# The down projection of a gated FFN, from a plain tiled product to Strassen's seven products, with its operands passed through DRAM

## The chip, the cores and the metric

The kernel runs on one core of one Trainium2 chip, in one launch. The metric is the device time of an execution in microseconds (us); lower is better. The engines are PE (TensorE, matrix products), DVE (VectorE), ACT (ScalarE), POOL (GpSimd) and SP (SyncE, which here only issues DMAs). An engine works through its own instructions in order; semaphores order the engines among themselves.

## The reference

One layer of a hybrid block over x of 1024 rows by 1024 columns, all in float32. What comes before the part that is changed is a combined input projection, forgetting attention (8 heads), an RWKV-7 recurrence (8 heads), their gated merge and an output projection. Then:

```
h2 = rmsnorm(x, g_ffn)
u = causal_dwconv(h2 @ w_up, conv_w, conv_b)              # w_up: 1024 x 5632, conv of width 3 along the rows
x = x + (gelu(u[..., :2816]) * u[..., 2816:]) @ w_down    # w_down: 2816 x 1024
ple_gate = sigmoid(rmsnorm(x, g_ple) @ w_ple_gate)        # w_ple_gate: 1024 x 1024
out = x + ple_gate * (p @ w_ple_up)
```

## The kernel before

Every float32 product is made of three matmuls of rounded parts: an operand is split into H (a cast to the fp32r format, on ACT) and L (the rest, a subtraction on DVE or POOL), and H·H, H·L and L·H are added up in PSUM. A function named `split` or `up_halve` makes such a pair.

The code gives instructions in a written order and with generators that take turns (`interleave`); a scheduler then sets each engine's order from dependences and its own estimate of times, so an instruction can be issued ahead of one that is written before it. Tiles are taken from pools; a tile of the same tag and place waits for the last reader of the one before it.

The stages in order of time: the first norm and projections (to about 380 us), attention head pair by head pair beside the next pair's projections (`fox_att`, `fox_z`, to about 660 us), the recurrence's chain beside gates (to about 960 us), the merge and the output projection `wout` with the second norm (to about 1110 us), the up projection `ffn_up` (to 1545 us), the down projection `ffn_down` (to 1814 us), and the gate projection `ple` (to the end).

The up projection is Strassen's scheme already: for each of 22 blocks f of 128 columns (and its partner f + 22) seven products over 512 rows and half the depth (`up_mul`, four steps of three matmuls of 128x512 each), from sums of weight quarters that POOL makes (`up_s12`, `up_s3`) and sums of the normed rows. DVE and ACT combine the products to c0 and c1, run the convolution (`up_conv`: one ACT and two DVE operations), gelu and the product u0·u1 (`up_m`), and store the block, 128 x 1024, to DRAM (`md`).

The down projection takes the 22 blocks in pairs. `down_load` brings two blocks of md and their rows of w_down from DRAM on SP's queue, `down_split` splits them, and `down` goes over eight row tiles and two column halves: six matmuls of 128x512 into one PSUM bank, then a DVE addition of the bank to the row tile of x (L1234, or L1236 for two banks). x was stored to DRAM (`x1d`) before the up projection and is loaded back by POOL's queue as the stage starts. In the last turn, three blocks are taken at once, and the third norm (`norm`: square and root on ACT, scaling on DVE, eight transposes on PE in `turn`, one split) follows two row tiles behind; the first gate products begin while the last norms run.

PSUM has eight banks of 128x512: in the up projection two "ps" and six "pu", in the down projection two "ps" and three "zt" of two banks each.

Of the kernel before, what the change touches and what calls it, by code (L numbers as in the profile page):

```python
# [29 lines left out]
NFB = DFF // P  # L30
RMS_EPS = 1e-6
# [53 lines left out]
class Net:  # L85
# [931 lines left out]
    def wout_w(self, ap, gp):  # L1017

        nc = self.nc
        W = []  # L1020
        for i in range(2):
            raw = gp.tile([P, 4, 256], F32, name=f"gB{i}", tag=f"gB{i}", bufs=1)
            nc.gpsimd.dma_start(raw, self.a["w_out"][i * 512:i * 512 + 512, 0:256].rearrange("(k p) n -> p k n", p=P))
# [51 lines left out]
    def up_load(self, f):  # L1075
        pool, tag = (self.wp, "wr") if f % 2 == 0 else (self.up, "rr")
# [90 lines left out]
    def up_m(self, f, c0, u1, q=None):  # L1167
        nc = self.nc
# [3 lines left out]
        (q or nc.sync).dma_start(self.md[f], u0)  # L1172

    def ffn_up(self, first, last):
# [9 lines left out]
        for f in range(NFB):  # L1184
            more = f + 1 < NFB
            c0 = up.tile([P, T], F32, name="c0", tag="c0", bufs=2)
            c1 = up.tile([P, T], F32, name="c1", tag="c1", bufs=2)
            m1 = mul(f, "a11", "b11") if f else first[0]
            nc.scalar.copy(c0[:, lo], m1)
            if f:  # L1190
                u1 = self.up_conv(before[1], NFB + f - 1)
            else:
                self.up_load(1)
            m2 = mul(f, "a12", "b21") if f else first[1]
            if f:
                self.up_m(f - 1, before[0], u1)
                self.up_rest(f)
# [3 lines left out]
            if f + 2 < NFB:  # L1201
                self.up_load(f + 2)
            m5 = mul(f, "s1", "t1")
            if more:
                self.up_a1(f + 1)
                self.up_s12(f + 1)
# [6 lines left out]
            if more:  # L1213
                self.up_halve(self.A[f + 1]["s2"], self.sums[f + 1][1][:])
                self.up_halve(self.A[f + 1]["s1"], self.sums[f + 1][0][:])
# [3 lines left out]
            if more:  # L1219
                self.up_s3(f + 1)  # L1220
            add(c0[:, hi], c0[:, hi], m3)  # L1221
            before = c0, c1
        u1 = self.up_conv(before[1], 2 * NFB - 1)
        self.up_m(NFB - 1, before[0], u1, nc.scalar)

    def down(self, ms, tb, z=None):

        ts = slice(tb * P, tb * P + P)
        for n in range(2):
            cs = slice(n * 512, n * 512 + 512)  # L1230
            ps = self.ps.tile([P, 512], F32, name="ps", tag="ps") if z is None else z[:, cs]
            self.mm3(ps, [((mh[:, ts], ml[:, ts]), (W[0][:, cs], W[1][:, cs])) for (mh, ml), W in ms])
            if z is None:
                self.nc.vector.tensor_add(self.x1[tb][:, cs], self.x1[tb][:, cs], ps)  # L1234
        if z is not None:
            self.nc.vector.tensor_add(self.x1[tb], self.x1[tb], z)  # L1236

    def down_first(self, pool):

        nc = self.nc  # L1240
        M = pool.tile([P, 4, T], F32R, name="hah", tag="hah", bufs=1)
        ms = []
        for f in range(2):
            W = self.wload(self.a["w_down"][f * P:f * P + P, :])
            raw = self.up.tile([P, T], F32, name="rr", tag="rr", bufs=2)
            nc.sync.dma_start(raw, self.md[f])
            mh, ml = M[:, 2 * f], M[:, 2 * f + 1]
            self.split(raw, mh, ml)
            ms.append(((mh, ml), (W[0][:, 0, :], W[1][:, 0, :])))
        return ms  # L1250

    def down_load(self, g):
        f0 = 2 * g
        raws = [self.wo.tile([P, 2, T], F32, name="vr", tag="vr", bufs=1)]
        self.nc.sync.dma_start(raws[0], self.a["w_down"][f0 * P:(f0 + 2) * P, :].rearrange("(k p) n -> p k n", p=P))
        for f in (f0, f0 + 1):
            raws.append(self.fp.tile([P, T], F32, name="uc", tag="uc", bufs=3))
            self.nc.sync.dma_start(raws[-1], self.md[f])
        return raws

    def down_split(self, g, raws, pools):
        H = self.wo.tile([P, 2, T], F32R, name="vh", tag="vh", bufs=2)
        L = self.wo.tile([P, 2, T], F32R, name="vl", tag="vl", bufs=2)
        if g < 10:
            pool, name = pools[g % 4]
            M = pool.tile([P, 4, T], F32R, name=name, tag=name, bufs=1)
        ms = []
        for j in range(2):
            f = 2 * g + j
            if f <= NFB - 4:  # L1270
                mh, ml = M[:, 2 * j], M[:, 2 * j + 1]
            else:
                mh, ml = [self.fp.tile([P, T], F32R, name=n, tag=n, bufs=3) for n in ("mh", "ml")]
                mh, ml = mh[:], ml[:]
            self.split(raws[1 + j], mh, ml)
            self.split(raws[0][:, j], H[:, j], L[:, j])
            ms.append(((mh, ml), (H[:, j], L[:, j])))
        return ms

    def ffn_down(self, ms, pools):  # L1280

        for g in range(1, NFB // 2):
            raws = self.down_load(g)
            for tb in range(NTB):
                if g == NFB // 2 - 1:
                    self.down(ms[:1], tb, self.zt.tile([P, T], F32, name="zt", tag="zt") if tb % 2 else None)
                else:

                    z = g == 1 and (tb < 3 or tb % 2)
                    self.down(ms, tb, self.zt.tile([P, T], F32, name="zt", tag="zt") if z else None)  # L1290
                if tb == 2:
                    after = self.down_split(g, raws, pools)
            ms = ms[1:] + after if g == NFB // 2 - 1 else after
        return ms
# [45 lines left out]
    def ple(self, q, tb, hT, pu, W):  # L1340
# [16 lines left out]
        elif tb % 4 == 3:  # L1357
            nc.gpsimd.dma_start(self.out[(tb - 3) * P:(tb + 1) * P, cs].rearrange("(b p) n -> p b n", p=P), self.sg)
# [7 lines left out]
    def body(self, stop):  # L1366
# [83 lines left out]
        self.tlag = 12.0  # L1450

# [20 lines left out]
        close_fwp()  # L1472
        close_gwp()
# [75 lines left out]
        self.wo, _ = self.pool("wo", side="right")  # L1549
# [3 lines left out]
        for cs in (slice(0, 256), slice(256, D)):  # L1553
            for tb in range(NTB):
                nc.gpsimd.dma_start(self.x1[tb][:, cs], self.a["x"][tb * P:tb * P + P, cs])
# [18 lines left out]
        self.md = self.tc.dram_tile([NFB, P, T], F32, name="md")  # L1574
# [27 lines left out]
        close_ps = self.pools(("ps", 2), ("pu", 6))  # L1602
# [31 lines left out]
        for tag, n, bufs in (("u", T, 2), ("s1r", 512, 1), ("s2r", 512, 1), ("s4r", 512, 1), ("s3r", 512, 1),  # L1634
                             ("c0", T, 2), ("c1", T, 2), ("rr", T, 2)):
            self.up.tile([P, n], F32, name=tag, tag=tag, bufs=bufs)
        ms = []
        self.ffn_up(first, lambda: ms.extend(self.down_first(hA)))
# [72 lines left out]
```

## Time and profile before

| | |
|---|---|
| runs | 1911.43, 1912.30, 1915.68 us; median 1912.3 |
| the profiled execution's own time | 1914.04 us |
| its span, first to last instruction | 1912.3 us |
| PE busy | 1843.1 us, 10999 matmuls |
| granted TensorE clock, mean | 0.987 |
| moved by DMA | 201.27 MB |

Rows of the timeline read: start, duration, engine, line of the kernel, operation, output<-inputs, count; in brackets, the idle time of the engine before it and what ended that. Rows that group instructions read: line, engine, operation, tiles, count, busy time and mean of one in ns, idle time before. Rows by stretch give each engine's busy time (and instructions), PE's granted clock, the share of the DMA engines' time and the GB/s moved. PEld is PE's weight load, which runs beside its matmuls.

### The profile page before, as it was taken

The numbers are of one execution on the slowest core, as the hardware profiler recorded it, in microseconds if no ns is written. First come the engines' busy times: TensorE is split into PE (matmuls) and PEld (weight loads), VectorE is DVE, ScalarE is ACT, GpSimd is POOL, SyncE is SP. The second block draws the span as 40 slices with busy tenths as digits, with TensorE's granted clock in tenths as the row PEclk, the third lists the DMA queues.
The fourth block names the chain that finished last, engine by engine and source line by source line (L and its number), as shares of the span: only waits on it lengthen the run. The fifth ranks groups of instructions, "written<-read, shape, count | busy, mean of one in ns | idle before, by whom it ended". The sixth has DMA issues, their size and how long they took to land.

```text
span 1912.3 us, 28229 instructions
## 1 busy us (share of the span) xinstructions
PE 1843.1 (96%) x10999; PEld 1507.3 (79%) x10999; DVE 1215.8 (64%) x2457; ACT 747.6 (39%) x1191; POOL 247.8 (13%) x195
## 2 busy tenths in 40 slices
PE   6999999899999999999999999999999979999999
PEld 5877779789897766666779978888888867778899
DVE  7446764676656434453362698888888867676843
ACT  4544333576757411222541353444343431121331
POOL 3000001000000000000054023333333200000000
PEclk9999999899999999999999999999999989999999
DMA  4356554322212355343654132222222273231041
GB/s 157 89 143 163 141 130 96 83 65 56 69 37 79 94 130 146 115 141 96 218 171 140 78 88 87 82 75 85 82 77 89 88 252 111 89 110 45 26 130 56
DMA packets 258429, 201.27 MB, mean 105 GB/s; under 512 B 77464, under 2 KB 227694, under 8 KB 258295
## 3 DMA queue, kind: packets, MB, share of 16 engines
q1 hardware_dynamic: 189943, 158.26, 27.3%
q10 hardware_dynamic: 65024, 28.61, 5.8%
q0 software_dynamic: 3328, 12.58, 1.9%
q8 instruction: 87, 1.43, 0.3%
q14 instruction: 47, 0.39, 0.1%
HBM read 142.23 MB, written 57.18 MB: 104 GB/s over the span
## 4 chain that ended last, share of the span: by engine, by line
PE 62%; DVE 4%; DMA 2%; ACT 2%; issue 1%; POOL 0%; SPq 0%; DVEq 0%; POOLq 0%; ACTq 0%
PE pu L1153 7%; PE pu L1155 7%; PE pu L1154 7%; PE zt L227 3%; PE zt L226 3%; PE zt L228 3%; PE ps L226 3%; PE ps L228 3%; PE ps L227 3%; PE zt L235 2%; PE zt L236 2%; PE zt L985 2%; PE zt L237 2%; PE zt L987 2%; PE zt L986 2%
## 5 line engine op out<-in xcount | busy, mean ns | idle before, releaser
L1234 DVE TENSOR_TENSOR x<-x,ps 128x512 f32<-128x512 f32 x142 | 96.4, 686 | 60.3 <-PE ps L228 60.1
L206 ACT CAST vh<-vr 128x1024 fp32r<-128x1024 f32 x32 | 32.1, 1047 | 184.0 <-PE ps L228 170.9
L206 ACT CAST wh<-wr 128x1024 fp32r<-128x1024 f32 (+1 forms) x45 | 40.2, 895 | 145.3 <-PE zt L236 85.6
L235 PE MATMUL zt<-hah,wh 128*128 128x512 f32 (+1 forms) x200 | 80.8, 405 | 0.0
L236 PE MATMUL zt<-hal,wh 128*128 128x512 f32 (+1 forms) x200 | 79.0, 395 | 0.0
L235 PE MATMUL zt<-hbh,wh 128*128 128x512 f32 (+1 forms) x200 | 78.7, 393 | 0.0
L237 PE MATMUL zt<-hah,wl 128*128 128x512 f32 (+1 forms) x200 | 78.2, 391 | 0.0
L236 PE MATMUL zt<-hbl,wh 128*128 128x512 f32 (+1 forms) x200 | 78.0, 390 | 0.0
L237 PE MATMUL zt<-hbh,wl 128*128 128x512 f32 (+1 forms) x200 | 77.6, 388 | 0.0
L1164 DVE SCALAR_TENSOR_TENSOR u<-c,par,u 128x1022 f32<-128x1022 f32 x44 | 73.6, 1672 | 0.8
L1163 DVE SCALAR_TENSOR_TENSOR u<-c,par,u 128x1023 f32<-128x1023 f32 x44 | 68.6, 1560 | 7.5 <-ACT u L1162 7.5
L1153 PE MATMUL pu<-hah,wh 128*128 128x512 f32 x176 | 70.3, 399 | 0.0
L1154 PE MATMUL pu<-hal,wh 128*128 128x512 f32 x176 | 69.8, 397 | 0.0
L1155 PE MATMUL pu<-hah,wl 128*128 128x512 f32 x176 | 69.7, 396 | 0.0
L1162 ACT ACTIVATE u<-c,par 128x1024 f32<-128x1024 f32 x44 | 54.7, 1242 | 28.3 <-DVE c L1221 28.3
L226 PE MATMUL zt<-vh,mh 128*128 128x256 f32 (+1 forms) x202 | 61.8, 306 | 0.0
L824 ACT ACTIVATE pr<-pr,st 128x128 f32<-128x128 f32 (+3 forms) x64 | 49.7, 777 | 30.7 <-DVE st L823 30.1
L228 PE MATMUL zt<-vh,ml 128*128 128x256 f32 (+1 forms) x202 | 61.2, 303 | 0.0
L227 PE MATMUL zt<-vl,mh 128*128 128x256 f32 (+1 forms) x202 | 61.0, 302 | 0.0
L848 DVE TENSOR_TENSOR pl<-tr,ph 128x512 fp32r<-128x512 f32 (+1 forms) x80 | 50.0, 633 | 14.5 <-ACT ph L847 13.9
L207 DVE TENSOR_TENSOR wl<-wr,wh 128x1024 fp32r<-128x1024 f32 (+1 forms) x36 | 39.5, 1100 | 24.0 <-ACT wh L206 23.7
L847 ACT CAST ph<-tr 128x512 fp32r<-128x512 f32 (+1 forms) x80 | 42.2, 542 | 19.7 <-PE tr L842 16.8
(549 smaller groups left out, 5767.6 us busy)
## 6 DMA issues: line engine op xcount, KB each, us to landing
X<-Xd SPq DMA_DIRECT2D x28, 448.0 KB
wr<-in_w_up SPq DMA_DIRECT2D x22, 512.0 KB
rr<-in_w_up SPq DMA_DIRECT2D x22, 512.0 KB
wr<-in_w_in ACTq DMA_DIRECT2D x21, 512.0 KB
md<-u SPq DMA_DIRECT2D x21, 512.0 KB
vr<-in_w_down SPq DMA_DIRECT2D x10, 1024.0 KB
uc<-md SPq DMA_DIRECT2D x20, 512.0 KB
gwr<-in_w_in ACTq DMA_DIRECT2D x11, 512.0 KB
```

Of the source, the lines that this page charges most:

```text
L206: self.nc.scalar.copy(h, r)
L226: nc.tensor.matmul(ps, lhsT=lh, rhs=rh, start=(i == 0), stop=False)
L227: nc.tensor.matmul(ps, lhsT=lh, rhs=rl, start=False, stop=False)
L228: nc.tensor.matmul(ps, lhsT=ll, rhs=rh, start=False, stop=(i == n - 1))
L235: nc.tensor.matmul(o, lhsT=H[:, k, :], rhs=hh[:, k, :], start=(k == 0), stop=False)
L236: nc.tensor.matmul(o, lhsT=H[:, k, :], rhs=hl[:, k, :], start=False, stop=False)
L237: nc.tensor.matmul(o, lhsT=L[:, k, :], rhs=hh[:, k, :], start=False, stop=(k == NKB - 1))
L1153: nc.tensor.matmul(ps, lhsT=wh[:, k, :], rhs=bh[:, k, :], start=k == 0, stop=False)
L1154: nc.tensor.matmul(ps, lhsT=wh[:, k, :], rhs=bl[:, k, :], start=False, stop=False)
L1155: nc.tensor.matmul(ps, lhsT=wl[:, k, :], rhs=bh[:, k, :], start=False, stop=k == 3)
L1164: nc.vector.scalar_tensor_tensor(u[:, 2:T], c[:, 0:T - 2], cw(0), u[:, 2:T], op0=ALU.mult, op1=ALU.add)
L1234: self.nc.vector.tensor_add(self.x1[tb][:, cs], self.x1[tb][:, cs], ps)
```

## The change

The down projection becomes Strassen's scheme with Winograd's sums. The 1024 rows, the 22 blocks of depth and the 1024 columns are each halved; the seven products have 512 rows, 11 blocks of depth and 512 columns.

The left operands: `ffn_up` goes over the blocks in the order `UP` (0, 11, 1, 12, ...), so that blocks i and 11 + i follow one another. After the second, POOL makes four sums of their halves (rows 0 to 511 and 512 to 1023), and seven pieces of 128x512 go to DRAM in place of two of 128x1024. The right operands: `down_sums` loads w_down's rows in pairs during attention, POOL makes four sums of each pair, and they are stored to DRAM (`wd2`). The products are then made one at a time over all 11 pairs, in steps of two pairs: `down_load` brings both operands of a step (512 KB each), `down_split` splits them, and four row tiles of six matmuls each run into four of the six "pu" banks, which stay open from the up projection on. When a product ends, its four banks are added to the rows and columns of x or of a buffer t that they belong to. Row tiles 0 to 3 of x are final after five products; their norm is made beside the last two. Row tiles 4 to 7 are normed after the last product, in turn with the gate products of row tiles 0 to 3.

DMAs that POOL's queue issued (a part of w_out, x twice, the output) are issued by SP's queue; the buffer for POOL's DMA descriptors is made smaller. x comes back into the place of the weight splits of the up projection instead of the place of its other tiles.

```diff
+UP = [f for i in range(NFB // 2) for f in (i, NFB // 2 + i)]
...
-            nc.gpsimd.dma_start(raw, self.a["w_out"][...
+            nc.sync.dma_start(raw, self.a["w_out"][...
...
     def up_conv(self, c, fb):
-        u = self.up.tile([P, T], F32, name="u", tag="u", bufs=2)
+        u = self.up.tile([P, T], F32, name="u", tag="u", bufs=3)
...
-    def up_m(self, f, c0, u1, q=None):
-        nc = self.nc
+    def up_m(self, f, c0, u1):
+        nc, gp, i = self.nc, self.nc.gpsimd, f % (NFB // 2)
+        lo, hi = slice(0, 512), slice(512, 1024)
+        dma = nc.sync.dma_start
         u0 = self.up_conv(c0, f)
         nc.scalar.activation(u0, u0, AF.Gelu_apprx_tanh)
         nc.vector.tensor_mul(u0, u0, u1)
-        (q or nc.sync).dma_start(self.md[f], u0)
+        if f == i:
+            dma(self.md["a11"][i], u0[:, lo])
+            self.um = u0
+            return lambda: None
+        v = self.um
+        s = self.up.tile([P, 3, 512], F32, name="sm", tag="sm", bufs=1)
+        gp.tensor_add(s[:, 0], v[:, hi], u0[:, hi])
+        gp.tensor_sub(s[:, 1], s[:, 0], v[:, lo])
+        gp.tensor_sub(s[:, 2], u0[:, lo], s[:, 1])
+        gp.tensor_sub(v[:, hi], v[:, lo], v[:, hi])
+        def store():
+            for n, r in (("a12", u0[:, lo]), ("a22", u0[:, hi]), ("s1", s[:, 0]), ("s2", s[:, 1]), ("s4", s[:, 2]),
+                         ("s3", v[:, hi])):
+                dma(self.md[n][i], r)
+        return store
...
+    DOWN = (("a11", "b11"), ("s2", "t2"), ("s1", "t1"), ("a12", "b21"), ("s4", "b22"), ("s3", "t3"), ("a22", "t4"))
+    def down_sums(self, pairs):
+        for i in pairs:
+            w = self.wt.tile([P, 2, D], F32, name="wt", tag="wt", bufs=1)
+            for j in range(2):
+                nc.sync.dma_start(w[:, j], self.a["w_down"][(j * H + i) * P:(j * H + i) * P + P, :])
+            yield 1.0
+            gp.tensor_sub(w[:, 0, lo], w[:, 0, hi], w[:, 0, lo])
+            gp.tensor_sub(w[:, 0, hi], w[:, 1, hi], w[:, 0, hi])
+            gp.tensor_sub(w[:, 1, hi], w[:, 1, hi], w[:, 0, lo])
+            gp.tensor_sub(w[:, 1, lo], w[:, 1, lo], w[:, 1, hi])
+            yield 1.0
+            for j, n in enumerate(("t1", "t3", "t4", "t2")):
+                nc.sync.dma_start(self.wd2[n][i], w[:, j // 2, j % 2 * 512:j % 2 * 512 + 512])
+            yield 1.0
...
+    def ffn_down(self, steps, ready, store, beside):
...
+        raws = {k: load(k) for k in (2, 3)}
+        store()
+        for tb in range(NTB):
+            nc.sync.dma_start(x[tb], self.x1d[tb])
+        ops = dict(enumerate(ready))
+        for k, (op, i, n) in enumerate(steps):
+            if i == 0:
+                ps = [self.pu.tile([P, 512], F32, name="pu", tag="pu") for _ in range(4)]
+            last = i + n == NFB // 2
+            AH, AL, BH, BL = ops.pop(k)
+            for tb in range(4):
+                ts = slice(tb * P, tb * P + P)
+                for j in range(n):
+                    f, l = i + j == 0, last and j == n - 1
+                    nc.tensor.matmul(ps[tb], lhsT=AH[:, j, ts], rhs=BH[:, j], start=f, stop=False)
+                    nc.tensor.matmul(ps[tb], lhsT=AH[:, j, ts], rhs=BL[:, j], start=False, stop=False)
+                    nc.tensor.matmul(ps[tb], lhsT=AL[:, j, ts], rhs=BH[:, j], start=False, stop=l)
...
+                if tb == 1:
+                    if k + 2 in raws:
+                        ops[k + 2] = split(raws.pop(k + 2))
+                    if k + 4 < len(steps):
+                        raws[k + 4] = load(k + 4)
+            if last:
+                m = self.DOWN.index(op)
+                for tb, p in enumerate(ps):
+                    if m == 0:
+                        nc.scalar.copy(t[:, tb], p)
+                        add(x[tb][:, lo], x[tb][:, lo], p)
+                    elif m in (1, 5):
+                        add(t[:, tb], t[:, tb], p)
+                    elif m == 2:
+                        add(x[tb][:, hi], x[tb][:, hi], p)
+                        add(x[tb + 4][:, hi], x[tb + 4][:, hi], p)
...
+            if op[0] in ("s3", "a22"):
+                next(beside, None)
...
                 interleave((att, 23.0), (self.fox_z(hp + 1, self.fox_w(hp + 1), zV), 31.5),
+                           (self.down_sums(range(hp * 4, min(hp * 4 + 4, NFB // 2))), 12.0),
...
+        def norm3():
+            hT.extend([self.htile(hA, "ha"), self.htile(hB, "hb")])
+            self.gain("g_ple", g)
+            W.append(self.ple_w0())
+            for i in range(2):
+                pu_load(self.ep, i, "pu0", 2)
+            for tb in range(4):
+                yield
+                yield
+                self.norm(tb, g, hT, xn[:, tb % 2, :], self.ep)
+        beside = norm3()
+        self.ffn_down(steps, ready, store, beside)
...
+        hi = iter(range(4, NTB))
+        for q in range(2):
+            for tb in range(4):
+                if q == 0:
+                    b = next(hi)
+                    self.norm(b, g, hT, xn[:, b % 2, :], self.ep)
+                self.ple(q, tb, hT, pu, W[q])
```

## Rows read from the trace of the kernel before

**Rows 1.** The page's first part: busy time, share of the span, instructions
```profile
PE 1843.1 (96%) x10999; PEld 1507.3 (79%) x10999; DVE 1215.8 (64%) x2457; ACT 747.6 (39%) x1191; POOL 247.8 (13%) x195
```
**Rows 2.** By stretch: up, start of down (two), down, attention
```profile
core 0: us, PE busy (x) PEld busy (x) DVE busy (x) ACT busy (x) POOL busy (x), PEclk, DMA share, GB/s
1200.00:1300.00 100.00, 100.00 (x431) 80.44 (x430) 84.93 (x93) 40.45 (x51) 32.30 (x20) 1.00 0.26 84
1560.00:1570.00 10.00, 1.84 (x9) 1.16 (x7) 0.76 (x1) 1.65 (x2) 0.00 (x0) 0.76 0.87 353
1570.00:1580.00 10.00, 6.62 (x18) 5.24 (x19) 10.00 (x12) 4.63 (x5) 0.00 (x0) 0.55 0.61 208
1680.00:1700.00 20.00, 19.85 (x86) 15.23 (x84) 15.07 (x20) 5.56 (x6) 0.00 (x0) 1.00 0.55 183
380.00:600.00 220.00, 217.79 (x1812) 192.92 (x1811) 143.95 (x425) 150.42 (x321) 14.34 (x7) 1.00 0.23 61
```
**Rows 3.** Waits, 1520 to 1610 us: total us, times, longest
```profile
PE ps L226 <- DVE x L1234: 12.5, 3, 11.5
```
**Rows 4.** Timeline of PE in the down projection, start to end
```profile
1544.75 0.40 PE L226 MATMUL ps<-wh,hah 128*128 128x512 f32 x1
...
1651.15 0.39 PE L226 MATMUL ps<-vh,hah 128*128 128x512 f32 x1
...
1653.67 0.39 PE L228 MATMUL ps<-vh,hah 128*128 128x512 f32 x1
...
1803.08 1.03 PE L283 MATMUL ps<-ident,vr 128*128 128x128 f32 x8
...
1813.10 1.03 PE L283 MATMUL ps<-ident,vr 128*128 128x128 f32 x8
1813.89 0.37 PE L226 MATMUL zt<-wh,hah 128*128 128x256 f32 x1
...
1814.21 0.28 PE L228 MATMUL zt<-wh,hal 128*128 128x256 f32 x1
...
1815.28 0.28 PE L228 MATMUL zt<-wh,hal 128*128 128x256 f32 x1
```
**Rows 5.** Timeline of DVE and POOL in up blocks, and DVE at its end
```profile
1305.59 0.69 DVE L1211 TENSOR_TENSOR c<-c,pu 128x512 f32<-128x512 f32 x1
...
1310.04 1.86 DVE L1163 SCALAR_TENSOR_TENSOR u<-c,par,u 128x1023 f32<-128x1023 f32 x1 [0.37 <-ACT u L1162]
...
1314.22 1.27 DVE L1163 SCALAR_TENSOR_TENSOR u<-c,par,u 128x1023 f32<-128x1023 f32 x1
...
1305.57 1.29 POOL L1109 TENSOR_TENSOR s2r<-s1r,rr 128x512 f32<-128x512 f32 x1
1309.14 1.68 POOL L1119 TENSOR_TENSOR s3r<-rr 128x512 f32<-128x512 f32 x1 [2.28 <-DVE vh L1100]
...
1552.53 1.22 DVE L1171 TENSOR_TENSOR u<-u 128x1024 f32<-128x1024 f32 x1
1553.67 1.22 DVE L207 TENSOR_TENSOR vl<-vr,vh 128x1024 fp32r<-128x1024 f32 x1
```
**Rows 6.** Timeline of ACT: the casts of two successive groups
```profile
1628.44 2.00 ACT L206 CAST vh<-vr 128x1024 fp32r<-128x1024 f32 x2 [19.02 <-PE ps L228]
...
1651.35 2.00 ACT L206 CAST vh<-vr 128x1024 fp32r<-128x1024 f32 x2 [19.02 <-PE ps L228]
```
**Rows 7.** Timeline of SP's queue, late in the up projection
```profile
1514.29 0.33 SPq L254 DMA_DIRECT2D wr<-in_g_ple  x1
1515.57 0.33 SPq L1172 DMA_DIRECT2D md<-u  x1
```
**Rows 8.** Groups by line (page), and one row of ACT's timeline
```profile
L1234 DVE TENSOR_TENSOR x<-x,ps 128x512 f32<-128x512 f32 x142 | 96.4, 686 | 60.3 <-PE ps L228 60.1
...
L1164 DVE SCALAR_TENSOR_TENSOR u<-c,par,u 128x1022 f32<-128x1022 f32 x44 | 73.6, 1672 | 0.8
L1163 DVE SCALAR_TENSOR_TENSOR u<-c,par,u 128x1023 f32<-128x1023 f32 x44 | 68.6, 1560 | 7.5 <-ACT u L1162 7.5
...
L848 DVE TENSOR_TENSOR pl<-tr,ph 128x512 fp32r<-128x512 f32 (+1 forms) x80 | 50.0, 633 | 14.5 <-ACT ph L847 13.9
...
1818.54 1.28 ACT L1352 ACT_TABLE_LOAD   x1
```

More of the change, by code (lines that the diff above doesn't have):

```diff
@@ L1219, in ffn_up @@
             if more:
-                self.up_s3(f + 1)
+                self.up_s3(more)
             add(c0[:, hi], c0[:, hi], m3)
             before = c0, c1
[L1223 to L1294, printed above, removed]
+        u1 = self.up_conv(before[1], NFB + f)
@@ new lines, in down_split, with down_first @@
+    def down_split(self, raws, tiles):
+        a, b, n = raws
+        AH, AL, BH, BL = tiles
+        for r, h, l in ((a, AH, AL), (b, BH, BL)):
+            self.split(r[:, 0:n], h[:, 0:n], l[:, 0:n])
+        return tiles
+    def down_first(self, pool, steps):
+        out = []
+        for name, (rp, tag), step in zip(("hah", "hal"), ((self.wp, "wr"), (self.up, "rr")), steps):
+            M = pool.tile([P, 4, 2, 512], F32R, name=name, tag=name, bufs=1)
+            a, b = [rp.tile([P, 2, 512], F32, name=tag, tag=tag, bufs=2) for _ in range(2)]
+            out.append(self.down_split(self.down_load(step, a, b), [M[:, j] for j in range(4)]))
+        return out
@@ new lines, in ffn_down, with load, split @@
+    def ffn_down(self, steps, ready, store, beside):
+        nc, dn = self.nc, self.dn
+        lo, hi = slice(0, 512), slice(512, 1024)
+        add = nc.vector.tensor_add
+        x = self.x1
+        def load(k):
+            return self.down_load(steps[k], *[dn.tile([P, 2, 512], F32, name=n, tag=n, bufs=2) for n in ("ra", "rb")])
+        def split(raws):
+            M = dn.tile([P, 4, 2, 512], F32R, name="op", tag="op", bufs=3)
+            return self.down_split(raws, [M[:, j] for j in range(4)])
+        raws = {k: load(k) for k in (2, 3)}
[15 more added lines that the diff above has]
+                    nc.tensor.matmul(ps[tb], lhsT=AL[:, j, ts], rhs=BH[:, j], start=False, stop=l)
+                if k == 2 and tb == 0:
+                    t = dn.tile([P, 4, 512], F32, name="t", tag="t", bufs=1)
+                if tb == 1:
[14 more added lines that the diff above has]
+                        add(x[tb + 4][:, hi], x[tb + 4][:, hi], p)
+                    elif m in (3, 4):
+                        cs = (lo, hi)[m - 3]
+                        add(x[tb][:, cs], x[tb][:, cs], p)
+                    else:
+                        add(x[tb + 4][:, lo], x[tb + 4][:, lo], p)
+                for tb in range(4):
+                    if m == 2:
+                        add(x[tb][:, hi], x[tb][:, hi], t[:, tb])
+                    elif m == 5:
+                        for cs in (lo, hi):
+                            add(x[tb + 4][:, cs], x[tb + 4][:, cs], t[:, tb])
+            if op[0] in ("s3", "a22"):
+                next(beside, None)
@@ L1357, in ple @@
         elif tb % 4 == 3:
[L1358 removed]
+            nc.sync.dma_start(self.out[(tb - 3) * P:(tb + 1) * P, cs].rearrange("(b p) n -> p b n", p=P), self.sg)
     def build(self, stop=99):
@@ L1450, in body @@
         self.tlag = 12.0
+        self.wt, close_wt = self.pool("wt", side="left")
+        self.wd2 = {n: self.tc.dram_tile([NFB // 2, P, 512], F32, name="wd" + n) for n in ("t1", "t2", "t3", "t4")}
         z_tile = lambda: self.zp.tile([P, 512], F32, name="z", tag="z")
```

122 lines of the change are left out of this document (71 added, 51 removed).

## The prediction, made before the changed kernel was run

> **What bounds the kernel now.** I read the page's first part, then the table by stretches, then who PE (TensorE) waited for, and last PE's own order of time where the down projection starts and ends. PE is busy 96% of the span [rows 1]. In the up projection (about 1110 to 1545 us) PE fills every microsecond and DVE (VectorE) 85% of them; in the down projection (1545 to 1814 us) PE is near full too, DVE at some 75%, and DMA at 0.55 where most is moved, except at the stage's start [rows 2]. There PE stands 11.5 us, the longest of its waits in that stretch, put down to a DVE addition to x [rows 3]; that addition has to have the residual rows back from DRAM, and the DMA share is then 0.87 at 353 GB/s [rows 2]. After it PE runs at the 1.2 GHz level for a while: 18 matmuls in 6.62 us, where 18 take 4.1 at 2.4 GHz; granted clock 0.55 over that stretch [rows 2]. So what decides is PE's count of matmuls, and next to it what PE stands for at the joints.
>
> **The products.** The down projection of before is 22 blocks x 8 row tiles x 2 halves x 3 split terms = 1056 matmuls of 128x512. It runs from 1544.75 to 1813.89, six transposing turns of 0.79 us for the third norm inside it: 269.1 us [rows 4]. A steady run of it has 11 steps in 2.52 us, 0.229 us each [rows 4]; the up projection has 431 in 100 us, 0.232 [rows 2]. 1056 x 0.229 + 4.7 is 246.5 us. The other 22.6 are the 11.5 us wait, 2.5 of slow clock behind it, and small waits on two accumulator banks: a group of 96 matmuls comes round every 22.91 us [rows 6], 0.9 over 96 x 0.229, some eight times. After, 7 products x 11 blocks x 4 row tiles x 3 terms = 924 matmuls. At 0.229 that is 211.6, at 0.232 214.4; with the same six turns 216.3 to 219.1. I take 218.1. **Gain before deductions: 269.1 - 218.1 = 51.0 us** (50.0 to 52.8), of which 30.5 are the 132 matmuls themselves and the rest the waits that the new order should not have: six accumulator banks stay open across the joint, and x is first needed when the first product ends, some 30 us in, rather than in the third row tile.
>
> **What can come back at the start of the stage.** Steps 0 and 1 are split during the last up block, as before, and give PE 2 x 24 x 0.231 = 11.1 us. Step 2 and 3 load into the space of t2 and beyond, free some 11 us before the up projection ends, so they should be there. Step 4 can be late: behind steps 2 and 3 SP's queue holds, as written, six stores of the last sums (which wait for POOL, some 15 us after PE has left the up projection: the last u product ends 9.0 us after it, and four sums of 1.29 us follow [rows 4, 5]), 4 MB of x, and then step 4: 6.5 MB at the 353 GB/s of the joint [rows 2] are 18 us, with splitting 36 us, needed at 22. That is a stall of up to 14 us and 2.5 of slow clock. Against it: SP's queue is not in the written order. The load of g_ple, written behind the whole down projection, was issued before the store of an up block [rows 7], so what is ready goes first, and x's new place (the up weights' splits, free as up ends) is ready before the sums. Between 0 and 16.5 I take **3**.
>
> **Supply and evacuation inside the stage.** Each step of 24 matmuls (5.5 us) now reads both operands anew, 1 MB: 190 GB/s. The nearest row moved 183 GB/s at a DMA share of 0.55, in smaller pieces (1 KB rows) [rows 2], so it fits, with two steps (11 us) from issue to use. Splits: per step two copies of 1.0 us on ACT (ScalarE) and two subtractions of 1.22 on DVE [rows 5, 6]; over the stage DVE does 88 us of splits, 32 accumulator additions of 0.69 [rows 8], 12 more without PSUM, and four norms: about 135 of 215. At a product's end the next has two spare banks (2.8 us); the third product ends with 12 additions, and a split may stand in front of them. Nothing to 1 us for each of seven ends: **2**.
>
> **The third norm.** Row tiles 0 to 3 are final after five of seven products and are normed beside the last two (33 us for four norms that come every 5.0 us now [rows 4]). At the end rows 4 to 7 remain; of the gate projection eight products of 24 x 0.119 = 2.9 us [rows 4] are ready as cover, 23 us for four norms. Against it ACT now changes between square root and sigmoid, 1.28 us for each table load [rows 8], up to eight of them. Nothing if PE's order puts the ready products first; 8 if the first norm stands alone (one such period, 5.0) and two or three table loads show: **3**.
>
> **The sums on POOL (GpSimd) in the up projection.** 11 pairs x 4 additions of 128x512, 1.29 us each alone [rows 5]: 5.2 us in 39.0 us (two up blocks of 84 x 0.232). POOL has room (32% busy). DVE is the question: a scalar_tensor_tensor that takes 1.27 us alone took 1.86 where a POOL addition ran into it, and that POOL addition 1.68 in place of 1.29; an addition from PSUM beside POOL kept its 0.69 [rows 5]. So operations with two SBUF operands shut each other out. DVE is busy 84.93% now [rows 2], 33.1 us of 39.0, waits on POOL included; if every new sum stopped it for its whole length, 38.3. It still fits, by 0.7 us. The sums can start when u's product is done, 10 us into a block, where three of DVE's next five operations are PSUM additions; the weight sums that queue behind them on POOL are made most of a block ahead of their use. Nothing to 1.3 us a pair (one blocked operation that reaches PE), 0 to 14 in all: **3**. The reordered blocks (i, 11 + i) and the third u buffer cost nothing by themselves: u's two halves are stored one after the other and the next u needs its place 10 us later.
>
> The Trainium skill, SBUF — State Buffer, section Who interferes with whom, has the same pair as an exclusive lock: whichever of a DVE instruction with two SBUF inputs and a GpSimd instruction that reads SBUF starts first holds it whole. The rows agree (1.86 against 1.27, and 0.69 unchanged). By that rule alone, all POOL time put on DVE, a pair would want 30.3 + 15.5 = 45.8 of 39.0 us, and the up projection would be 75 us longer; the rows show why it need not: the four present additions in a block, 5.2 us, cost DVE 1.4, by the means of its two conv lines, 1.56 and 1.67 for 1.27 alone [rows 5, 8].
>
> **The weight sums in attention.** 44 more POOL operations and 22 MB of DMA between 380 and 600 us, where PE is 99% busy, DVE 65%, POOL 7%, DMA 0.23 [rows 2]. DVE's operations there mostly read PSUM, like its costliest, the split of the transposed weights [rows 8]. The 22 MB add about 100 GB/s to 61. SP's queue gets 66 more entries, and behind a store that waits for POOL stand the loads of the triangular solve and the small attention stores, none needed within some tens of us, and the rows of the decay sums, which are double buffered. 0 to 6: **2**. The DMAs moved from POOL's queue to SP's (w_out, x twice, the output) I put at nothing: their transfers are the same, they lie beside PE work as the first ones do now, and if that cover goes each is a few us of waiting, within the bounds given.
>
> **Sum.** 51 - (3 + 2 + 3 + 3 + 2) = 38 us. The profiled execution took 1914.0 (span 1912.3), the median of the runs is 1912.3, 1.7 less. 1914.0 - 38 - 1.7 = 1874.3; I say **1875**.
>
> **Rivals.**
> 1. The order of SP's queue is as written: step 4 waits for stores and x. Price 16.5 instead of 3: 1888. For: in before the same stretch starved PE for 11.5 us. Against: SP's order in [rows 7].
> 2. All gains and no deductions: 1860.
> 3. The up projection becomes DVE's, and this one ends slower. Place: the block that makes the sums; conv, gelu and product of u stand in order on ACT and DVE, and if the four sums come to lie ahead of the next block's weight sums and each stops a two-operand operation, PE waits for the split weights. Price: all 5.2 us of a pair, 11 times, is 57 against the 3 taken: 1914.0 - 51 + 10 + 57 - 1.7 = 1928. From 41 us in all (3.7 a pair) it decides the sign. Against: DVE's 0.7 us of room even then and six banks. By the Trainium skill's lock rule alone (SBUF — State Buffer, Who interferes with whom) it would be 1946, with the same small chance.
> 4. The change doesn't do what it says because DMA, not PE, sets the pace of the seven products. 44.6 MB would have to come at under 209 GB/s to matter (213 us) and at under 173 to turn the sign; 183 GB/s at share 0.55 makes full rate some 330.
>
> **How the numbers follow.** The forecast (0 to 16 us of deductions beyond or below its 13, 1860 to 1888) has 0.70; rival 1 and other stalls of that size 0.15; rival 2 0.05; rival 3, whole or in part, 0.07; rival 4 0.03. The forecast's own range with rivals 1 and 2 is 1860 to 1890; with half of rival 3 (28 us in the up projection, 1899) I give **1860 to 1897**, which leaves out the rest of 3 and most of 4, and some of the tails. A measurement of this kernel tells about 0.2% (4 us) from no change. Faster 0.90: all of 1, 2 and the forecast, less a little for several stalls together; within 0.2%: 0.03; slower 0.07, from 3 and 4.
>
> **What would show it.** Right: 924 matmuls of 128x512 at 0.229 to 0.233 us in some 220 us; no PE wait over 5 us where up ends, and the clock at 1.0 there; the up block still at 19.5 us; POOL near 45% in it; DMA share about 0.6 through the products; a few us of PE waits at the last product's end. Wrong: an up period above 19.8 us, PE waiting for a copy that waited for DMA at steps 4 to 6, waits on x's additions at each product's end, or an attention stretch longer than before.

## The result, and the profile after

The changed kernel takes 1892.5 us (median of 1885.65, 1892.12, 1892.91 and 1893.18) against 1912.7 before, a ratio of 0.9884 [0.9858, 0.9910]: faster by 1.2%, 17.5 us more than the 1875 forecast and inside the range. The profiled execution took 1885.65 (span 1883.8, before 1912.3), so its trace has 28.5 us less. Executions of one kernel differ here by some 8 us (the kernel before 1909.31 to 1916.83 in one set of runs); where two traces of the changed kernel could be compared (experiment 1) the difference lies ahead of the up projection.

By stretch, the changed kernel: the up projection, the two ready steps of the down projection, the hole behind them, the clock's return, and the products.

```profile
core 0: us, PE busy (x) PEld busy (x) DVE busy (x) ACT busy (x) POOL busy (x), PEclk, DMA share, GB/s
1500.00:1540.00 40.00, 40.00 (x173) 32.18 (x172) 34.40 (x37) 15.76 (x21) 13.39 (x9) 1.00 0.29 99
1552.00:1562.00 10.00, 10.00 (x46) 8.24 (x45) 6.85 (x6) 2.31 (x2) 1.59 (x2) 1.00 0.55 208
1562.00:1576.00 14.00, 1.41 (x7) 0.83 (x5) 1.17 (x1) 2.02 (x2) 3.43 (x3) 0.65 0.84 298
1576.00:1580.00 4.00, 3.83 (x9) 2.58 (x10) 3.68 (x4) 2.16 (x3) 0.00 (x0) 0.53 0.97 342
1580.00:1600.00 20.00, 20.00 (x90) 16.56 (x89) 10.29 (x13) 10.48 (x14) 0.00 (x0) 1.00 0.93 303
1600.00:1700.00 100.00, 100.00 (x443) 82.81 (x442) 56.94 (x62) 38.17 (x41) 0.00 (x0) 1.00 0.61 196
```

Once past the hole the products run full: 443 matmuls in 100 us, 0.226 us each, where the up projection has 431 [rows 2]. But the hole where the stage begins is still there, as long as before. PE's waits in the whole stage, and SP's queue ahead of the long one:

```profile
PE pu L1326 <- ACT op L207: 12.7, 1, 12.7
PE zt L227 <- DVE x L1351: 0.8, 1, 0.8
PE ps L284 <- DVE xn L291: 0.6, 1, 0.6
```
```profile
1546.70 7.10 SPq L1315 DMA_DIRECT2D x<-x1d  x5
1560.22 0.80 SPq L1191 DMA_DIRECT2D mda<-u  x2
1561.64 4.13 SPq L1191 DMA_DIRECT2D mds<-sm  x3
1565.83 0.42 SPq L1191 DMA_DIRECT2D mds<-u  x1
1566.31 0.94 SPq L1315 DMA_DIRECT2D x<-x1d  x2
1567.29 0.46 SPq L1279 DMA_DIRECT2D ra<-mda  x1
1567.79 0.47 SPq L1280 DMA_DIRECT2D rb<-in_w_down  x1
```

The first load of step 2 (`ra`) is issued at 1567.29, 4 us after PE has run out of ready steps (1563.3), behind seven of the eight loads of x and the six last stores. The longest wait of before was 11.5 [rows 3]; this one is 12.7, at another place and for another reason, and in the 4 us behind it the granted clock is 0.53 (0.55 in [rows 2]).

The other loss is early. The first and last start of the up projection's first line, in the kernel before and in the changed kernel:

```profile
L1153 PE MATMUL pu<-hah,wh x176: 394/394/792, 1104.1 to 1530.1; 128*128 128x512 f32 x176
L1155 PE MATMUL pu<-hah,wh x176: 394/394/793, 1111.7 to 1537.7; 128*128 128x512 f32 x176
```

The up projection takes 426.0 us in both and starts 7.6 us later. From the first matmul of the down projection to the end the trace went from 367.5 us (1912.3 - 1544.75) to 331.5 (1883.8 - 1552.33): 36.1 less, of which 7.6 are lost again ahead of it.

### The profile page after: what moved, and what is told of

Same layout as the page of the kernel before. It is cut to its first block, busy times and chain, and to the rows that moved or that the text cites. A ratio compares the mean times of both kernels' runs of the same rounds, so it can differ in the third digit from the quotient of the medians.

```text
span 1883.8 us, 28328 instructions
## 1 busy us (share of the span) xinstructions
PE 1808.4 (96%) x10867; PEld 1485.2 (79%) x10867; DVE 1201.8 (64%) x2382; ACT 783.1 (42%) x1236; POOL 354.8 (19%) x251
## 3 DMA queue, kind: packets, MB, share of 16 engines
q1 hardware_dynamic: 230071, 220.40, 37.7%
## 4 chain that ended last, share of the span: by engine, by line
PE 64%; DVE 3%; ACT 2%; DMA 1%; issue 1%; POOL 0%; SPq 0%; ACTq 0%; POOLq 0%; DVEq 0%
PE pu L1155 7%; PE pu L1157 7%; PE pu L1156 7%; PE pu L1326 3%; PE pu L1327 3%; PE pu L1328 3%; PE zt L228 3%; PE zt L229 3%; PE zt L227 3%; PE zt L236 2%; PE zt L237 2%; PE zt L986 2%; PE zt L238 2%; PE zt L988 2%; PE zt L987 2%; PE yps L636 1%
## 5 line engine op out<-in xcount | busy, mean ns | idle before, releaser
L1326 PE MATMUL pu<-op 128*128 128x512 f32 x292 | 114.5, 393 | 12.7 <-ACT op L207 12.7
L1327 PE MATMUL pu<-op 128*128 128x512 f32 x292 | 114.3, 391 | 0.0
L1328 PE MATMUL pu<-op 128*128 128x512 f32 x292 | 114.2, 391 | 0.0
L208 DVE TENSOR_TENSOR op<-ra,op 128x1024 fp32r<-128x1024 f32 (+1 forms) x40 | 45.1, 1128 | 72.1 <-ACT op L207 71.8
L207 ACT CAST op<-ra 128x1024 fp32r<-128x1024 f32 (+1 forms) x40 | 39.1, 978 | 118.3 <-PE pu L1328 87.0
L1165 DVE SCALAR_TENSOR_TENSOR u<-c,par,u 128x1023 f32<-128x1023 f32 x44 | 72.7, 1652 | 4.3 <-ACT u L1164 4.1
L1326 PEld LDWEIGHTS pu<-op 128*128 128x128 f32 x292 | 55.1, 189 | 24.5 <-ACT op L207 13.1
L1327 PEld LDWEIGHTS pu<-op 128*128 128x128 f32 x292 | 55.2, 189 | 12.0 <-DVE op L208 0.8
L1328 PEld LDWEIGHTS pu<-op 128*128 128x128 f32 x292 | 55.1, 189 | 11.5
```

Source lines behind the costliest of these rows:

```text
L207: self.nc.scalar.copy(h, r)
L1165: nc.vector.scalar_tensor_tensor(u[:, 1:T], c[:, 0:T - 1], cw(1), u[:, 1:T], op0=ALU.mult, op1=ALU.add)
L1326: nc.tensor.matmul(ps[tb], lhsT=AH[:, j, ts], rhs=BH[:, j], start=f, stop=False)
L1327: nc.tensor.matmul(ps[tb], lhsT=AH[:, j, ts], rhs=BL[:, j], start=False, stop=False)
L1328: nc.tensor.matmul(ps[tb], lhsT=AL[:, j, ts], rhs=BH[:, j], start=False, stop=l)
```

## The experiments

Each was run beside the kernel before on the same chip. Two questions: why PE still stands where the stage begins (2 and 8), and what the weight sums cost and why (3 to 7, 9 to 12). Times are medians.

**1. The changed kernel once more.** No edit.

> The changed kernel once more, nothing altered. Its own runs were 1885.65 once and 1892.1 to 1893.2 three times. If the 7 us between them are the chip's (another chip, another moment), this run keeps to one of the two levels and its trace shows which stretch is longer than in the profiled execution; if they are the kernel's own (an order that two engines settle by chance), both levels come back on this chip too.

1889.43 us (1887.01 to 1893.14), ratio 0.9878 [0.9854, 0.9902]. Not two levels but a spread over 6 us. Its trace has the up projection from 1117.4, 5.7 us later than the first trace; from there to the end both take 772 us (1889.3 - 1117.4 and 1883.8 - 1111.7). So what differs between these two traces arises ahead of the up projection. Experiments 2 and 8 leave the early code as it is too, and their up projections start at 1122.3 and 1114.4: one trace alone says where it starts to within some 5 us. This run is the control for all that follows.

**2. Steps 2 and 3 out of the up projection's pool.**

```
+        self.dr, close_dr = self.pool("dr", side="left")      # ahead of pool "dn"
-   *[dn.tile([P, 2, 512], F32, name=n, ...) for n in ("ra", "rb")]
+   *[self.dr.tile([P, 2, 512], F32, name=n, ...) for n in ("ra", "rb")]
         def split(raws, k):
+            if k in (2, 3):     # operands of steps 2 and 3 in t2's place
+                M = self.hb.tile([P, 4, 2, 512], F32R, name=("hbh", "hbl")[k - 2], ...)
```

> The raw weights of the steps get a pool of their own, which lies where t2 was, and the split operands of steps 2 and 3 lie in t2's space too, so that nothing of these two steps shares a pool with the tiles of the up projection. Theory A (space): step 2 was late because its pool as a whole waits until the last up tiles are given back; then PE does not stand where the down projection starts, the 12.7 us wait and some 2.5 us of slow clock behind it go, and the time is 13 to 16 us under the changed kernel's, 1870 to 1879, unless step 4 is late in its place, which would leave 5 to 14 us of a wait a step later. Theory B (bandwidth): x, 4 MB, and the weights together are what PE waits for; then the wait stays over 8 us, wherever it comes to lie, and the time is within 5 us of the changed kernel's.

1887.86 us, 0.9876 [0.9848, 0.9903]: no gain that can be measured (from the start of the up projection to the end its trace has 771.0 us, with 771.9 in experiment 1). The wait went to step 4. PE's waits, then SP's queue:

```profile
PE pu L1330 <- ACT op L207: 10.7, 1, 10.7
```
```profile
1556.50 0.46 SPq L1279 DMA_DIRECT2D ra<-mda  x1
...
1559.39 1.22 SPq L1319 DMA_DIRECT2D x<-x1d  x2
1573.17 1.52 SPq L1191 DMA_DIRECT2D mda<-u  x2
1575.45 5.04 SPq L1191 DMA_DIRECT2D mds<-sm  x3
1580.55 0.42 SPq L1191 DMA_DIRECT2D mds<-u  x1
1581.06 3.23 SPq L1319 DMA_DIRECT2D x<-x1d  x6
1584.39 0.42 SPq L1279 DMA_DIRECT2D ra<-mda  x1
```

Theory A was right about the space: step 2 is now issued at 1556.50, 6.6 us before the down projection's first matmul (1563.1), and PE has 48 more matmuls without a wait. But step 4 stands behind the six stores and six loads of x, is issued at 1584.39, and PE waits 10.7 us for it. That is rival 1 of the prediction, at the step that it named; in the changed kernel an earlier step met the same queue. Theory B stays open: the wait is over 8 us too.

**3. Without the weight sums.** `down_sums` is not called; the steps read plain rows of the down weights for t1 to t4, so the products aren't the reference's.

> The weight sums are left out: no additions of them on POOL, no loads and no stores for them; in their place the steps read rows of the down weights of the same size, so that the seven products use other operands than the reference's. What they cost from the start to the up projection is then seen whole: if the 7.4 us by which the up projection starts later than before are theirs, it starts at 1104 to 1106 and the time is 6 to 8 us under the changed kernel's; if something else shifted (the pool made for them, another order of SP's queue), it starts at 1109 or later and the time moves by under 3 us.

1877.07 us (1873.03 to 1878.51), 0.9806 [0.9780, 0.9833]: 12.4 us under experiment 1.

```profile
L1155 PE MATMUL pu<-hah,wh x176: 394/394/792, 1103.6 to 1529.3; 128*128 128x512 f32 x176
```

The up projection starts half a microsecond before that of the kernel before. So the whole early loss, and more than the 7.6 us of the first trace, is the weight sums'.

**4. The weight sums not before the attention stage.** Their buffer comes from that stage's pool (`self.fp.tile(... "wt")`).

> The weight sums take their buffer from the pool of the attention stage, so that they can't begin before that stage, where they are written; the sums themselves are unchanged. If their cost was that they ran ahead, beside the first norm and the first stage, where DMA and POOL are wanted, the first stage ends as before the change (near 310 us and not 315) and the up projection starts at 1104 to 1108, 4 to 8 us earlier than in the changed kernel. If they cost the same wherever they lie (DVE and POOL shutting each other out, DMA), the loss moves to the attention and the up projection starts at 1110 to 1114; packed closer there, it could be more.

1894.80 us, 0.9903 [0.9882, 0.9923], 5.4 over experiment 1: no better, and as the intervals overlap not clearly worse. The first stage did recover (its last projection starts at 309.5, with 316.2 in experiment 1 and 313.4 without sums), but the attention lost more: between 400 and 500 us PE is busy 89.5 us instead of 97.0, POOL 39.7 instead of 16.5, and the up projection starts at 1121.5. Running ahead wasn't the fault.

**5. Only the transfers of the sums.** The four `gp.tensor_sub` are left out; t1 to t4 hold plain rows.

> Of the weight sums only the transfers are left, the same loads and stores; POOL's 44 operations are left out, so that the four summed operands are plain rows of the down weights and not the reference's. Without the sums altogether the time fell by some 12 us and the up projection began at 1103.6 (1111.7 and 1117.4 with them). If the cost is DVE and POOL shutting each other out of SBUF, it goes with POOL's operations: 1876 to 1881, up projection from 1103 to 1107. If it is the transfers (22 MB beside the loads of the first stages), it stays: 1886 to 1893, up projection from 1111 to 1118.

1877.48 us, 0.9804 [0.9788, 0.9821]; the up projection starts at 1105.0. The 22 MB cost nothing that can be measured.

**6. Only POOL's operations.** One buffer of zeros, no loads, no stores; t1 to t4 are plain rows again.

> The other half: POOL's 44 operations stay, on one buffer of zeros, and the loads and stores of the weight sums are left out; the steps read rows of the down weights of the same size in place of the summed operands, so the products use other operands than the reference's. If POOL's operations cost (locking DVE out), 1886 to 1893; if the transfers do, 1876 to 1881, up projection from 1103 to 1107. Without loads to wait for POOL's work may lie closer together than in the changed kernel; a cost in between would be put to that.

1891.02 us, 0.9879 [0.9861, 0.9897]; the up projection starts at 1119.5. Together with experiment 5 this shows that the cost is POOL's 44 operations. With nothing to wait for they all lie between 28 and 92 us, and the loss is nearly complete there: matmuls that stand at 60 to 160 us in experiment 3 come some 14.8 us later here (medians). DVE's groups by form up to 640 us, first without sums (experiment 3), then with POOL's operations alone, then the changed kernel (experiment 1):

```profile
L523 DVE TENSOR_TENSOR tT<-tT,tt 128x110 f32<-128x110 f32 x12 | 3.2, 271 | 0.3
L1459 DVE TENSOR_SCALAR nx<-nx,nst 128x1024 f32<-128x1024 f32 x4 | 3.0, 751 | 0.3
L246 DVE TENSOR_TENSOR nst<-nst 128x1 f32<-128x1 f32 x8 | 2.0, 253 | 0.1
```
```profile
L246 DVE TENSOR_TENSOR nst<-nst 128x1 f32<-128x1 f32 x8 | 6.1, 768 | 0.1
L1458 DVE TENSOR_SCALAR nx<-nx,nst 128x1024 f32<-128x1024 f32 x4 | 6.1, 1517 | 0.3
L523 DVE TENSOR_TENSOR tT<-tT,tt 128x110 f32<-128x110 f32 x12 | 3.3, 271 | 0.3
```
```profile
L523 DVE TENSOR_TENSOR tT<-tT,tt 128x110 f32<-128x110 f32 x12 | 5.4, 448 | 0.3
L1459 DVE TENSOR_SCALAR nx<-nx,nst 128x1024 f32<-128x1024 f32 x4 | 3.0, 751 | 0.3
```

A DVE operation on one element a partition goes from 253 to 768 ns where POOL's additions lie beside it; in the changed kernel others are struck, those of the triangular solve. Over all 1104 DVE instructions ahead of the chain (each form's change of mean, times its count) DVE's own durations grew by some 17 us in this run and by 12 in experiment 1; the up projection starts 15.9 and 13.8 us later than in experiment 3. The other traces go along, roughly: 10 and 8.1 in the first one of the changed kernel, 14 and 18.7 in experiment 2, 0.8 and 1.4 in experiment 5. The Trainium skill, SBUF — State Buffer, section Who interferes with whom, says that the one that comes second is blocked for the other's whole instruction. The rows agree: a POOL addition takes 1.29 us [rows 5], and the longest of the eight one-element operations 1.27, so a tiny operation can pay for a big one. Which ones pay depends on which instructions meet.

In the changed kernel the first stage loses little: against experiment 3 (313.4) its last projection starts 1.2 us late in the first trace and 2.8 in experiment 1, and the chain's first matmul (663.5 there) 8.6 and 12.8. Most of it goes where attention begins: between 340 and 440 us PE is busy 94.5 us without sums, 88.2 and 87.1 with them. PE's longest wait there, in experiments 3 and 1:

```profile
PE z L917 <- DVE ft L909: 2.4, 1, 2.4
```
```profile
PE z L917 <- DVE ft L909: 5.6, 1, 5.6
```

In experiment 6, where no sum stands at that place, nothing more is lost there.

**7. The sums beside the recurrent chain.** The `down_sums` generator is interleaved with `chain()` and `gates()`, in a buffer of that stage.

> The weight sums, unchanged, are made beside the recurrent chain (about 670 to 900 us), in a buffer of that stage, where POOL stood idle but for fills and the DMA share was 0.48. If what they cost was their place among the stages that wait for DVE and DMA, the up projection starts at 1104 to 1107 and the time is 8 to 12 us under the changed kernel's, 1879 to 1884. If 22 MB or POOL's work cost the same anywhere, the chain's stage is longer by 6 us or more and nothing is won.

1894.20 us, 0.9901 [0.9886, 0.9916], and nothing won. Up to the chain the trace is that of experiment 3 (first chain matmul 662.2, there 663.5); then chain lines that ran for 230.6 us take 250.5. PE's waits from 640 to 760 us:

```profile
PE yps L636 <- DMA X<-Xd: 7.0, 3, 5.3
PE ch L628 <- DMA TT<-Wd: 3.3, 2, 2.2
PE yps L649 <- DVE X L630: 2.0, 1, 2.0
```

Without sums the first two are 1.4 each. Both wait for loads, so the sums' transfers on SP's queue may have a part in these 20 us beside POOL's operations; the two were not told apart here. An idle POOL says nothing about a stage where each result is waited for.

**8. Stores and x away from SP's queue.** Experiment 2, and:

```
-                dma(self.md[n][i], r)                       # six stores of the last pair
+                (nc.gpsimd.dma_start if f == NFB - 1 else dma)(self.md[n][i], r)
-            nc.sync.dma_start(x[tb], self.x1d[tb])
+            nc.gpsimd.dma_start(x[tb], self.x1d[tb])
```

> As in the run with early operands for steps 2 and 3, and the last pair's six stores and the loads of x go to POOL's queue, behind the sums that the stores wait for anyway, so that on SP's queue step 4 stands behind steps 2 and 3 alone. Theory A2 (the order of one queue: what stands behind the stores and x is late, whichever step that is): the 10.7 us wait before step 4 goes as well, no PE wait over 3 us in the first 40 us of the down projection, and the time is 13 to 17 us under the changed kernel's, 1873 to 1878. Theory B (bandwidth: x, stores and operands are together more than DMA moves in that time): steps 4 to 7 are issued early but land late, PE waits 5 us or more in all at them, and under 10 us are won.

1881.82 us (1877.29 to 1884.01), 0.9830 [0.9813, 0.9848]: 9.2 us better than experiment 1 by the ratios (0.0048 of 1912). PE's waits, SP's queue and the stretch:

```profile
PE pu L1330 <- ACT op L207: 3.2, 1, 3.2
PE pu L1331 <- DVE op L208: 0.9, 1, 0.9
```
```profile
1548.30 0.46 SPq L1279 DMA_DIRECT2D ra<-mda  x1
...
1561.48 0.37 SPq L1279 DMA_DIRECT2D ra<-mda  x1
```
```profile
1560.00:1580.00 20.00, 16.81 (x75) 13.58 (x73) 6.95 (x7) 4.98 (x6) 11.28 (x12) 1.00 0.97 347
```

Step 4 goes out at 1561.48, 6.6 us after the stage's first matmul (1554.9), and the 10.7 us wait shrinks to 4.1 (granted clock 1.00 here, 0.91 in the next 20 us). So the queue's order was most of it (theory A2), and what is left agrees with theory B: the DMA share is 0.97 at 347 GB/s. The gain is under the 13 to 17 expected. Whether the queue alone would have done, without the places of experiment 2, was not run.

**9. The sums between chain and up projection, on POOL.** On top of 8, in steps after each `merge_rwkv`.

> On top of the run with the stores and x on POOL's queue (1881.8): the weight sums on POOL lie between the chain and the up projection (about 900 to 1100 us), where PE was 99% busy, DVE 43% and no recurrence waits. POOL makes splits of weights there that PE needs. If the sums cost only where DVE's answer is waited for at once, the up projection starts some 215 us after the chain's last matmul as before, and the 10 to 13 us come back: 1869 to 1873. If POOL's splits come late behind them, or DVE is shut out of what PE waits for, the stretch grows by what it saves: 1878 to 1890.

1919.51 us, 1.0043 [1.0028, 1.0058]: slower than the kernel before. PE's longest wait is 19.2 us for a split of w_out, and SP's queue shows why:

```profile
1048.34 4.56 SPq L1265 DMA_DIRECT2D wdt<-wt  x4
1052.94 0.92 SPq L1631 DMA_DIRECT2D x<-in_x  x2
1054.95 0.80 SPq L1257 DMA_DIRECT2D wt<-in_w_down  x2
1055.81 0.42 SPq L216 DMA_DIRECT2D vr<-in_w_out  x1
```

w_out's load is issued at 1055.81, behind sums' stores and loads that wait for POOL and for each other; in experiment 8 it goes out at 1022.76. From the chain's last matmul to the up projection it is 258 us (896.6 to 1154.8) instead of 210 in experiment 3. That wait is a part of these 48 us; POOL's splits of weights, which I had put as the rival, are another (three waits, 6.4 us), and the rest was not taken apart.

**10. The same on DVE.** `gp.tensor_sub` becomes `nc.vector.tensor_sub`.

> The same place, the 44 additions on DVE instead of POOL, at about 0.69 us each (a DVE operation with two SBUF operands of that size took 0.690) 30 us of DVE where it has 115 free of 200. No second engine reads the operands' SBUF beside it. Expected 1869 to 1873, as good as on POOL or better; if POOL's place costs by its queue or by shutting DVE out, this one is 4 us or more under it.

1900.08 us, 0.9932 [0.9919, 0.9944]. Better than on POOL by 19 us, with the same wait for w_out still 9.9 us. Expectation missed, as far as that wait shows for the same reason.

**11. The sums in the changed kernel's places, on DVE.** On top of 8.

> On top of the run with the stores and x on POOL's queue (1881.8): the weight sums in the changed kernel's places, with DVE doing the additions. If what cost was POOL and DVE shutting each other out (57 us of POOL's operations), 30 us of DVE's own should cost under 6: 1870 to 1876. If DVE's time as such is what those stages lack, the loss stays 8 to 14: 1878 to 1884.

1880.73 us (1875.61 to 1881.69), 0.9828 [0.9811, 0.9844], the same as experiment 8; the up projection starts at 1113.7 (there 1114.4). DVE's other instructions keep their durations now (0.7 us in all by the same working), but its own 44 additions of 0.69 us are 30 us. Half the time, hardly any blocking, and the same loss: blocking is not needed for it. DVE is busy only 65% of the attention [rows 2], so its share of busy time doesn't show the loss either; that DVE's time is short where a result is waited for fits both, but is argued and not shown.

**12. The sums inside the up projection, on POOL.** On top of 8, in halves of 256 columns, in a buffer of the up projection's pool.

> On top of the run with the stores and x on POOL's queue (1881.8): the weight sums are made inside the up projection, on POOL, in halves of 256 columns (88 operations of some 0.7 us, about 60 us, from its first block on), where PE sets the pace with 6 banks, POOL was 44% busy and DVE 91%. Theory P (what the sums cost is set by whether PE waits for DVE's or POOL's next result there; the up projection has operands made a block ahead): the up projection starts at 1103 to 1106 and still takes 426 us from its first matmul to the first one of its last block, 1869 to 1873. Rival 3 of the prediction (DVE and POOL shut each other out, the up projection becomes DVE's, with 60 us more of POOL's work in some 14 blocks): it grows by 15 to 40 us, 1886 to 1910. The loads of the up weights behind stores that wait for POOL would show as PE waits for the split weights.

1926.63 us, 1.0066 [1.0053, 1.0079]. The first half of theory P held (the up projection starts at 1106.2), the second did not: the stage grew by 53.9 us.

```profile
L1155 PE MATMUL pu<-hah,wh x176: 393/394/796, 1106.2 to 1586.1; 128*128 128x512 f32 x176
```

Rival 3's size, but not its mechanism, as this run's waits (1110 to 1400 us) and a stretch of it show:

```profile
POOL wt L1264 <- DMA wt<-in_w_down: 63.7, 15, 7.3
...
ACT u L1164 <- POOL sm L1185: 43.8, 4, 11.4
DVE u L1165 <- ACT u L1164: 43.0, 5, 11.7
```
```profile
1200.00:1300.00 100.00, 83.04 (x329) 65.72 (x329) 66.58 (x68) 29.20 (x38) 67.33 (x57) 0.89 0.51 164
```

DVE isn't full but emptier (66.6 us of 100; 91.0 in experiment 8), and its conv lines take no longer (1666 ns against 1711). POOL stands 63.7 us, in 15 waits, before a sum whose load hasn't landed; behind it in its queue stand the sums of u, which keep the u buffers, which ACT waits for, and then DVE and PE.

## Why the prediction was right, and where not

Direction and range held; the likeliest value was 14 to 18 us low, and the gain 20.2 us where 37.7 were forecast. That it still lies in the range is partly luck: two terms were too small by some 17 us in the first trace, and 8 us of others were not needed. Term by term:

- **The products.** 218.1 with six turns. Measured: 229.7 us with four turns (1552.33 to 1782.02), less 14.9 for the hole is 214.8, and 216.4 with the two turns that moved behind it. A little under the forecast, with hardly any of the 2 taken for supply and product ends: PE waits at none of the first six ends and 0.8 us at the last (for the addition to x), and the DMA share of 0.61 is the one forecast.
- **The start of the stage: the step that failed.** 3 of 0 to 16.5 taken; measured 14.9: from 1563.02 to 1580.17 PE starts 10 matmuls, 2.3 us' worth, in 17.15 us, of which 12.7 are the wait and some 2 the slow clock. I held rival 1 for unlikely because one load in [rows 7] had overtaken a store, and I placed step 2 safely in t2's space. The overtaking is real, but it follows what the tiles' space allows: as I read the code the pool of the raw weights also covers tiles of the up projection, and giving it a place of its own moved the loads (experiment 2). Rival 1's price, 16.5, came within 1.6, but it was worked out for step 4; the wait came at step 2 in the changed kernel and at step 4 as soon as step 2 was mended, so the number's closeness is luck and the mechanism, one queue's order, is not. Experiment 8 shows that order to be most of it. It puts the last stores and the loads of x on POOL's queue, where x had been before the change: the DMAs moved to SP's queue, which the prediction put at nothing, are a part of this loss (in experiment 2 six loads of x stand 3.2 us ahead of step 4); stores and x were not moved one by one.
- **The weight sums: the second one.** 2 of 0 to 6 taken; measured 12.4 (experiments 1 and 3), 8.1 in the first trace against experiment 3. Six of the eleven pairs were made before 160 us, in stages that I hadn't priced, but that was not the fault: 1.2 and 2.8 us are lost up to 316 us, and most goes from 340 to 440, where the other five stand and attention begins. What was wrong is the kind of cost: I looked for DVE's big operations and for DMA; it was POOL's operations (experiments 5 and 6), beside which small DVE ones got longer, while the 22 MB were free.
- **The sums of u on POOL.** 3 of 0 to 14 taken; measured 0: 426.0 us before and after, though DVE's busy time rose to 91 in 100 (84.93 in [rows 2]). Rival 3's mechanism did not show here; experiment 12 shows that this stage can lose as much by a wait in POOL's queue.
- **The third norm.** 3 taken; what follows the products grew from 98.4 to 101.8 us, 1.6 of it the two turns, so 1.8.

In the first trace this adds up: 38 forecast, less 11.9 at the start and 5.6 for the sums beyond what I took, plus 3.7 for products and supply, 3 for the sums of u and 1.2 for the norm that weren't needed, is 28.4; the span fell by 28.5. The stretches are the whole span, so such a sum must close: it shows where the time went, not why. With 12.4 for the sums in place of 7.6 the forecast would have been 1889.4, which is also experiment 1's median.

What stays open: how the 12 us divide between blocked DVE instructions and DVE's mere lack of time. Experiment 11 has next to none of the one and as much loss. And no place was found where the sums are free; with their transfers off SP's queue, the stretch between chain and up projection was not tried.

## What to carry to other kernels

When work leaves a stage's PE time and goes to an idle engine, price it by what waits for a result at that place, not by how idle the engine is: an idle POOL took the sums at a cost of 12 us in the early stages, 20 beside the chain (experiment 7), and 54 where it stood waiting for a load ahead of sums that others needed (experiment 12). At a joint of stages, list for each queue what the first late load stands behind, stores that wait for arithmetic above all, and expect that mending one step hands the wait to the next (experiment 2) until the queue itself is cleared (experiment 8). Look at which space a buffer's pool covers: here step 2's loads went out 15 us after the stage's first matmul from a pool over the space of the stage before, and 6.6 us ahead of it from a pool of their own.

## What the runs showed that I had not expected

The seven products ran at 443 matmuls in 100 us of full clock, the up projection at 431 to 432 with the same shape of matmul; no run here says why. And 44 additions of 512 columns, written in the same places, cost 12 us on POOL, and moved to DVE at half the duration each they left the kernel's time where it was (experiments 8 and 11).
